# The FFN's last projection: VectorE in written order, free banks first in the third part, GpSimd's share given to VectorE

## The chip, the core and the metric

The kernel runs on one core of a Trainium2 chip. TensorE (PE in the profile) multiplies, VectorE (DVE) and ScalarE (ACT) do elementwise work, GpSimd (POOL) helps them, and the queue of SyncE (SP) issues the loads. Each engine works through its own list of instructions, and semaphores order work between engines. The metric is the device time of one execution in microseconds; the median of three runs of the kernel before is 882.91 us (882.73 to 884.14).

## What is computed

One layer of a streaming encoder on 512 tokens of 1024 features, in float32. Only the last lines are touched by the change: `h` is the residual after attention and recurrence, `w_ffn_out` has 2816 rows.

```python
hn = rmsnorm(h, norm_ffn_g[l])
gu = jnp.einsum('bsd,de->bse', hn, w_ffn_in[l])
g, up = jnp.split(gu, 2, axis=-1)
h = h + (jax.nn.silu(g) * up) @ w_ffn_out[l]
return rmsnorm(h, final_norm_g)
```

## The kernel before

A float32 operand is held as two float32r numbers, a high part (ScalarE's copy, line 82) and the rest (VectorE's subtraction of that copy, line 83). A product of two such operands is three matmuls (`mm3`, lines 76 to 78). So each tile of weights or activations that TensorE reads costs one ScalarE and one VectorE instruction first: `split`. A tile that is first made by a sum (VectorE) and then split goes VectorE, ScalarE, VectorE.

The last projection multiplies activations (512 tokens, four tiles `t` of 128, by 2816 features) with `w_ffn_out`. Its 22 feature tiles are taken in 11 pairs `i`. Pairs 0 to 5, `plain`, are multiplied directly. Pairs 6 to 10, `paired`, go through a seven-product block scheme in place of eight products: the blocks are two halves of the tokens by two feature tiles, and two feature tiles by two halves of the columns. `left` and `right_` are split blocks, or sums of blocks, of the activations; `t12`, `t3b` and `t4` are split sums of blocks of the weights (`out_sums`).

TensorE's order is written out by hand inside `tc.manual_schedule`. It has seven parts: 1. plain pairs, first column half (weights `fo0_0` to `fo0_5`); 2. paired, `fo0_6` to `fo0_10`; 3. plain pairs 0 to 2, second column half (`fo1_0` to `fo1_2`); 4. `t12`; 5. plain pairs 3 to 5 (`fo1_3` to `fo1_5`); 6. `t3b`; 7. `t4`. Sums are kept in PSUM banks: four `po` for the plain pairs, two `pq` and two `qq` for the block products. Each part ends with VectorE's additions of banks to `h` (`h_add`, and `h_out`, which also squares the sum on ScalarE with `accum_out` and multiplies it by the final gain). After part 2 the four `po` banks are used again for the second column half: banks of tokens 2 and 3 are free after part 1, those of tokens 0 and 1 only after part 2.

In the kernel before, the order of the other engines comes from the framework's scheduler, which goes by its own estimate of times; where an instruction stands in an engine's list is then fixed in the program. Tiles come from pools with a few buffers each (weights four and three, raw loads three), and a load waits until the buffer's last reader is done. `weights(name, ahead)` issues loads and splits for `ahead` chunks beyond the one asked for; `spread` hands out listed preparations one or two at a time.

GpSimd's share before: the low parts of the activations of pairs 0, 1, 2 and 4 in `split_act`, and the gain product of tokens 0 and 1 in the first column half (`h_out(..., pool, ...)`).

Of the kernel before, what the change touches and what calls it, by code (L numbers as in the profile page):

```python
# [38 lines left out]
def block_kernel(ctx: ExitStack, tc: tile.TileContext, x, norm_mix_g, w_in, b_merge, rel_table,  # L39
# [28 lines left out]
    def f(ap):  # L68
        return ap.bitcast(F32)
# [999 lines left out]
    def split_act(i):  # L1069
        o = act2[i]  # L1070
        pl, bufs = (acp, 13) if i == 0 else (ohp, OUT_TILES)
        hi = pl.tile([P, 2, S], F32R, tag="act", bufs=bufs, name=f"act_hi{i}")
        lo = acp.tile([P, 2, S], F32R, tag="act", bufs=13, name=f"act_lo{i}")
        act.activation(hi[:], o[:], AF.Copy)  # L1074
        (pool if i in (0, 1, 2, 4) else dve).tensor_sub(lo[:], o[:], f(hi[:]))  # L1075
        for c in range(2):
            actT[2 * i + c] = (hi[:, c], lo[:, c])

# [30 lines left out]
    def a_first(i):  # L1109
        o, left[i] = act2[i], pair_tile(i, "left")  # L1110
        split(left[i][:, :, 0], left[i][:, :, 1], o[:, :, 0:256])

    def a_sums(i):
        o, right_[i] = act2[i], pair_tile(i, "right")
        s = tg_.tile([P, 2, 256], F32, tag="tg", name=f"s_{i}")
        a11, a12, a21, a22 = (o[:, c, t * 256:t * 256 + 256] for t in range(2) for c in range(2))
        dve.tensor_add(s[:, 1], a21, a22)
        dve.tensor_sub(s[:, 0], s[:, 1], a11)
        dve.tensor_sub(a11, a11, a21)
# [15 lines left out]
    def out_block(o, lhs, which, a, w, k, start, at=every):  # L1135
        toks = slice(a * P, (a + 1) * P)
        mm3(o, lhs[:, which, 0, toks], lhs[:, which, 1, toks], w(0, k, at), w(1, k, at), start, False, parts=True)

    def h_add(cc, t, po, at=every):
        hs = ht[t][:, cc * S + at.start:cc * S + at.stop]  # L1140
        dve.tensor_add(hs, po, hs)

    def h_out(cc, t, po, eng, i, at):

        n = slice(cc * S + at.start, cc * S + at.stop)
        hs = ht[t][:, n]
        dve.tensor_add(hs, po[:, 0:at.stop - at.start], hs)  # L1147
        junk = tg_.tile([P, S], F32, tag="tg", name=f"oj{t}_{i}")
        act.activation(junk[:, 0:at.stop - at.start], hs, AF.Square, accum_out=osq[t][:, i:i + 1])
        eng.tensor_mul(hs, hs, g_fin[:, n])  # L1150

    def out_norm(t, parts):

# [18 lines left out]
    def bank(tag, name):  # L1172
        return ps.tile([P, S], F32, tag=tag, bufs=4 if tag == "mm" else 2, name=name)

    def spread(todo, n):

        for _ in range(min(n, len(todo))):
            todo.pop(0)()

    half = N_PLAIN // 2  # L1180
    with tc.manual_schedule(engines={mybir.EngineType.PE}):

        todo = [lambda i=i: a_first(i) for i in paired]
        po = [bank("mm", f"po_out0_{t}") for t in range(NT)]
        for i in plain:
            if i:
                split_act(i)
# [3 lines left out]
            spread(todo, 1)  # L1191
        spread(todo, len(todo))
        for t in (2, 3):
            h_add(0, t, po[t][:])
        pq = [bank("s", f"p_out{a}") for a in range(2)]
        for n, i in enumerate(paired):
            w = weights(f"fo0_{i}", 4)
            for a in range(2):
                out_block(pq[a][:], left[i], 0, a, w, 0, n == 0)
            for a in range(2):  # L1200
                out_block(po[a][:], left[i], 1, a, w, 1, False)
            a_sums(i)
        for a in range(2):
            h_add(0, a, pq[a][:])
            h_out(0, a, po[a], pool, 0, every)
        todo = [lambda i=i: a_second(i) for i in paired]
        po = [bank("mm", f"po_out1_{t}") for t in range(NT)]
        for i in plain[:half]:
            w = weights(f"fo1_{i}", 4)
            for t in range(NT):  # L1210
                out_pair(po[t], t, i, w)
            spread(todo, 2)
        spread(todo, len(todo))

        qq = [bank("t", f"q_out{a}") for a in range(2)]
        for n, i in enumerate(paired):
            w = weights(f"t12_{i}", 4)
            for a in range(2):
                out_block(pq[a][:], right_[i], 0, a, w, 0, False)
            for a in range(2):  # L1220
                out_block(qq[a][:], right_[i], 1, a, w, 1, n == 0)
        for a in range(2):
            h_add(1, a, pq[a][:])
            h_add(1, 2 + a, qq[a][:])
        todo = [lambda i=i: a_last(i) for i in paired]
        for i in plain[half:]:
            w = weights(f"fo1_{i}", 4)
            for t in range(NT):
                out_pair(po[t], t, i, w)
            spread(todo, 2)  # L1230
# [58 lines left out]
```

## Time and profile before

| | us |
|---|---|
| median of three runs | 882.91 |
| the profiled execution | 883.89 |
| its span, first to last instruction | 882.1 |
| TensorE busy in it | 863.6 (98%) |
| VectorE busy | 594.3 (67%) |
| ScalarE busy | 485.9 (55%) |
| GpSimd busy | 112.8 (13%) |

Of the three numbers at the start of a timeline's row the first is the start in us from the span's begin, the second the busy time; a bracket at its end gives the idle time of the engine before it and who ended it. TensorE starts a 128x512 matmul every 0.227 us in the rows although each is shown as 0.39 us long, since matmuls overlap: distances are taken from starts. The table by stretches gives busy time and count per engine and then the granted TensorE clock. The last projection starts at 746.8 us in the span, and its first block of the change at 755.8 us.

### The profile page before, as it was taken

Reading aid. Unit: us, or ns where it says so; the run is one execution under the profiler, and the core shown is the slowest. Engines: PE = TensorE matmul, PEld = TensorE weight load, DVE = VectorE, ACT = ScalarE, POOL = GpSimd, SP = SyncE. Lnnn points to the kernel's source line nnn. Section 1 sums busy time; section 2 is a strip of 40 time slices with the busy share of each in tenths; the row PEclk is TensorE's granted clock in tenths of the full one; section 3 lists DMA queues with packets and bytes.
Section 4 is the critical chain, followed back from the end, with each engine's and each line's share of the span. In section 5 each row is a group of like instructions: output and inputs, shape, how many; then the busy total and the mean of one; then the engine's idle time right before and its main releaser. Section 6 shows DMA issues by size and latency. Waiting matters only on the chain.

```text
span 882.1 us, 13360 instructions
## 1 busy us (share of the span) xinstructions
PE 863.6 (98%) x5139; PEld 768.0 (87%) x5139; DVE 594.3 (67%) x928; ACT 485.9 (55%) x857; POOL 112.8 (13%) x170
## 2 busy tenths in 40 slices
PE   8999999999999999999999999999999999897997
PEld 6988888888889888898888889999999999785886
DVE  5666556663456675766557458888887885888655
ACT  7676556642257675766534367565555655633314
POOL 3612112120112132322000000000000001301000
PEclk9999999999999999999999999999999999998999
DMA  8133232433332332322324532333343332536502
GB/s 288 52 120 99 93 91 79 118 96 96 107 108 72 88 92 74 108 84 61 95 94 155 181 96 72 120 96 97 97 126 113 96 97 95 175 124 199 165 7 95
DMA packets 88303, 95.34 MB, mean 108 GB/s; under 512 B 5696, under 2 KB 74912, under 8 KB 88240
## 3 DMA queue, kind: packets, MB, share of 16 engines
q1 hardware_dynamic: 86640, 90.98, 33.1%
q10 hardware_dynamic: 1376, 3.47, 1.1%
q8 instruction: 40, 0.66, 0.3%
q14 instruction: 23, 0.19, 0.1%
q0 software_dynamic: 224, 0.05, 0.0%
HBM read 92.34 MB, written 2.14 MB: 107 GB/s over the span
## 4 chain that ended last, share of the span: by engine, by line
PE 88%; DVE 6%; ACT 2%; DMA 1%; issue 1%; POOL 1%; DVEq 0%; ACTq 0%; POOLq 0%
PE p_fu L78 2%; PE p_fg L78 2%; PE p_fg L77 2%; PE p_fg L76 2%; PE p_fu L77 2%; PE p_fu L76 2%; PE pT L872 2%; PE o L892 2%; PE po_v L76 2%; PE po_v L78 2%; PE po_v L77 2%; PE po_xr L76 2%; PE po_xr L77 2%; PE po_gr L76 2%; PE po_k L76 2%; PE po_gr L78 2%
## 5 line engine op out<-in xcount | busy, mean ns | idle before, releaser
L861 POOL TENSOR_SCALAR p<-p,rl 128x128 f32<-128x128 f32 (+1 forms) x64 | 36.9, 596 | 134.7 <-DVE rl L859 134.4
L1075 POOL TENSOR_TENSOR act_lo<-act,act_hi 128x1024 fp32r<-128x1024 f32 x4 | 10.5, 2629 | 332.9 <-ACT act_hi L1074 327.0
L76 PE MATMUL po_out<-whl_fo,act_hi 128*128 128x512 f32 x96 | 38.7, 403 | 6.4 <-DVE h L1147 5.9
L858 ACT ACTIVATE p<-p,m 128x128 f32<-128x128 f32 (+1 forms) x64 | 35.7, 560 | 12.1 <-DVE m L857 11.8
L78 PE MATMUL po_out<-whl_fo,act_lo 128*128 128x512 f32 x96 | 38.0, 395 | 1.8 <-POOL act_lo L1075 1.8
L77 PE MATMUL po_out<-whl_fo,act_hi 128*128 128x512 f32 x96 | 37.9, 395 | 0.0
L76 PE MATMUL po_v<-whl_v,xnT 128*128 128x256 f32 x128 | 36.5, 285 | 0.0
L78 PE MATMUL po_v<-whl_v,xnT 128*128 128x256 f32 x128 | 36.2, 283 | 0.0
L77 PE MATMUL po_v<-whl_v,xnT 128*128 128x256 f32 x128 | 36.2, 283 | 0.0
L83 DVE TENSOR_TENSOR whl_qk<-raw_qk,whl_qk 128x1024 fp32r<-128x1024 f32 x16 | 20.9, 1306 | 13.4 <-ACT whl_qk L82 13.4
L857 DVE CUSTOM_DVE_ANT_0 p<-s,bias 128x128 f32<-128x128 f32 (+1 forms) x64 | 29.1, 484 | 1.0 <-PE s L849 1.0
L76 PEld LDWEIGHTS po_out<-whl_fo,act_hi 128*128 128x128 f32 x96 | 18.4, 191 | 11.7 <-DVE h L1147 7.1
L83 DVE TENSOR_TENSOR whl_fu_s<-s_fu,whl_fu_s 128x1024 fp32r<-128x1024 f32 x20 | 24.1, 1222 | 6.2 <-ACT whl_fu_s L82 6.2
L83 DVE TENSOR_TENSOR pp<-pT,pp 128x384 fp32r<-128x384 f32 (+1 forms) x48 | 27.5, 596 | 0.5 <-ACT pp L82 0.4
L77 PE MATMUL po_xr<-xnT,whl_xr 128*128 128x512 f32 (+1 forms) x80 | 27.7, 353 | 0.0
L77 PE MATMUL po_gr<-xnT,whl_gr 128*128 128x512 f32 (+1 forms) x80 | 27.5, 347 | 0.0
L78 PE MATMUL po_gr<-xnT,whl_gr 128*128 128x512 f32 (+1 forms) x80 | 27.3, 347 | 0.0
L78 PE MATMUL po_xr<-xnT,whl_xr 128*128 128x512 f32 (+1 forms) x80 | 27.2, 346 | 0.0
L76 PE MATMUL po_gr<-xnT,whl_gr 128*128 128x512 f32 (+1 forms) x80 | 27.1, 347 | 0.0
L83 DVE TENSOR_TENSOR whl_fg_s<-s_fg,whl_fg_s 128x1024 fp32r<-128x1024 f32 x20 | 24.0, 1222 | 4.2 <-ACT whl_fg_s L82 4.0
L76 PE MATMUL po_xr<-xnT,whl_xr 128*128 128x512 f32 (+1 forms) x80 | 26.3, 351 | 0.4 <-ACT xnT L534 0.4
L83 DVE TENSOR_TENSOR whl_fo<-raw_fo,whl_fo 128x1024 fp32r<-128x1024 f32 x17 | 20.6, 1220 | 9.0 <-ACT whl_fo L82 9.0
(496 smaller groups left out, 3240.9 us busy)
## 6 DMA issues: line engine op xcount, KB each, us to landing
raw_fg<-in_w_ffn_in_dram SPq DMA_DIRECT2D x24, 512.0 KB, 4.0
raw_fu<-in_w_ffn_in_dram SPq DMA_DIRECT2D x22, 512.0 KB, 3.7
raw_fo<-in_w_ffn_out_dram SPq DMA_DIRECT2D x17, 512.0 KB, 3.6
raw_qk<-in_w_in_dram SPq DMA_DIRECT2D x32, 256.0 KB, 3.2
raw_xr<-in_w_in_dram SPq DMA_DIRECT2D x8, 512.0 KB, 3.9
raw_gr<-in_w_in_dram SPq DMA_DIRECT2D x8, 512.0 KB, 3.8
raw_ga<-in_w_in_dram SPq DMA_DIRECT2D x8, 512.0 KB, 3.5
raw_gb<-in_w_in_dram SPq DMA_DIRECT2D x8, 512.0 KB, 3.5
```

The costliest lines, as they stand in the source:

```text
L76: pe.matmul(o, sh, mh, start=start, stop=False, skip_group_check=parts)
L77: pe.matmul(o, sh, ml, start=False, stop=False, skip_group_check=parts)
L78: pe.matmul(o, sl, mh, start=False, stop=stop, skip_group_check=parts)
L83: dve.tensor_sub(lo, src, f(hi))
L857: dve.tensor_tensor_reduce(prob[qb][:], scs[qb][:, 0:w], bias[:, S - w:S], -1.0, 3e38, ALU.add, ALU.min, nmax[:, qb:qb + 1])
L858: act.activation(prob[qb][:], prob[qb][:], AF.Exp, bias=nmax[:, qb:qb + 1], scale=-1.0, accum_out=lsum[:, qb:qb + 1])
L861: pool.tensor_scalar(prob[qb][:], prob[qb][:], rl[:, qb:qb + 1], 1.0, ALU.mult, ALU.mult)
L872: pe.transpose(pt[:, at * P:(at + 1) * P], prob[qb][:, kb * P:(kb + 1) * P], ident[:])
L892: pe.matmul(po[:, S - n:S], st, pp[i][:, part, lo:lo + n], start=kb == 0 and part == 0, stop=kb == NT - 1 and part == 1)
L1075: (pool if i in (0, 1, 2, 4) else dve).tensor_sub(lo[:], o[:], f(hi[:]))
```

## The change

Five things are done to the last projection alone.

1. VectorE's instructions are put under the hand-written order too, so that within this block they stand in the program as the code says. The code is written in another order: `split_act`, `a_first`, `a_sums`, `a_second` and `a_last` stand where VectorE is to do them.
2. GpSimd keeps only `split_act(0)`. The low parts of pairs 1, 2 and 4 and the two gain products (`h_scale`) go to VectorE.
3. In part 3 the first two plain pairs are multiplied for tokens 2 and 3 first, then for tokens 0 and 1.
4. `weights` looks 3 (or 2) chunks ahead where it was 4.
5. The gain products of tokens 0 and 1 move from the end of part 2 into part 5, and the `t4` sums and splits stand ahead of the closing additions.

The diff, cut:

```diff
-        (pool if i in (0, 1, 2, 4) else dve).tensor_sub(lo[:], o[:], f(hi[:]))
+        (dve if i else pool).tensor_sub(lo[:], o[:], f(hi[:]))
...
-    with tc.manual_schedule(engines={mybir.EngineType.PE}):
+    with tc.manual_schedule(engines={mybir.EngineType.PE, mybir.EngineType.DVE}):
...
+            if i + 2 in plain:
+                split_act(i + 2)
+            if n < len(paired):
+                a_first(paired[n])
+            if n:
+                a_sums(paired[n - 1])
...
-            w = weights(f"fo0_{i}", 4)
+            w = weights(f"fo0_{i}", 3)
...
             h_add(0, a, pq[a][:])
-            h_out(0, a, po[a], pool, 0, every)
+            h_sum(0, a, po[a], 0, every)
...
+        first_two = [weights(f"fo1_{i}", 2) for i in plain[:2]]
+
+        for ts in ((2, 3), (0, 1)):
+            for i, w in zip(plain[:2], first_two):
+                for t in ts:
+                    out_pair(po[t], t, i, w)
+        for i in plain[2:half]:
+            w = weights(f"fo1_{i}", 3)
...
-        todo = [lambda i=i: a_last(i) for i in paired]
+        todo = [lambda i=i: a_last(i) for i in paired] + [lambda a=a: h_scale(0, a, dve, every) for a in range(2)]
...
+        ws = [weights(f"t4_{i}", 5) for i in paired]
         for a in range(2):
             h_out(1, 2 + a, pq[a], dve, 0, every)
...
-        ws = [weights(f"t4_{i}", 5) for i in paired]
```

What this does to VectorE's list is shown at three places. The names: `act_lo` is the low part of a plain pair, `whl_...` a split weight tile, `left`/`right` split activations, `s` their sums, `h0` to `h3` the residual of a token tile, `raw_t3b` and `t2` sums of weight blocks.

VectorE at the start of the block, after the last product of the stage ahead (line 1087); before:

```order
L1087 TENSOR_TENSOR act20_7499<-act20_7499,c_u20_7379 128x1024
L83 TENSOR_TENSOR left6_7663<-act12_6523,left6_7663 128x2x256
L1119 TENSOR_TENSOR act12_6523<-act12_6523 128x256
L1120 TENSOR_TENSOR act12_6523<-act12_6523,s_6_7870 128x256
L83 TENSOR_TENSOR whl_fo0_4_7670<-raw_fo0_4_0_7671,whl_fo0_4_7670 128x1024
```

The same place now:

```order
L1087 TENSOR_TENSOR act20_7499<-act20_7499,c_u20_7379 128x1024
L1075 TENSOR_TENSOR act_lo1_7630<-act2_5308,act_hi1_7629 128x1024
L83 TENSOR_TENSOR whl_fo0_2_7633<-raw_fo0_2_0_7634,whl_fo0_2_7633 128x1024
L83 TENSOR_TENSOR whl_fo0_3_7638<-raw_fo0_3_0_7639,whl_fo0_3_7638 128x1024
L1075 TENSOR_TENSOR act_lo2_7668<-act4_5551,act_hi2_7667 128x1024
```

The low part of pair 1 was GpSimd's and now stands right behind that product on VectorE; two weight splits that stood ahead of the product stand behind it.

VectorE at the end of part 2 and the start of part 3, where the additions into `h0` and `h1` free the two banks that TensorE needs; before:

```order
L83 TENSOR_TENSOR left9_7771<-act18_7252,left9_7771 128x2x256
L1141 TENSOR_TENSOR h0_4500<-p_out0_7845,h0_4500 128x512
L83 TENSOR_TENSOR whl_t12_8_8038<-raw_t12_8_8039,whl_t12_8_8038 128x512
L265 TENSOR_TENSOR raw_t12_9_8079<-raw_t12_9_8079 128x512
L1141 TENSOR_TENSOR h1_4501<-p_out1_7846,h1_4501 128x512
L83 TENSOR_TENSOR whl_t12_8_8038<-t2_8_8043,whl_t12_8_8038 128x512
L1147 TENSOR_TENSOR h0_4500<-po_out0_0_7625,h0_4500 128x512
L265 TENSOR_TENSOR raw_t12_10_8119<-raw_t12_10_8119 128x512
```

The same place now:

```order
L83 TENSOR_TENSOR whl_fo1_2_7955<-raw_fo1_2_0_7956,whl_fo1_2_7955 128x1024
L1141 TENSOR_TENSOR h0_4500<-p_out0_7890,h0_4500 128x512
L1146 TENSOR_TENSOR h0_4500<-po_out0_0_7625,h0_4500 128x512
L1141 TENSOR_TENSOR h1_4501<-p_out1_7891,h1_4501 128x512
L1146 TENSOR_TENSOR h1_4501<-po_out0_1_7626,h1_4501 128x512
L265 TENSOR_TENSOR raw_t12_6_7985<-raw_t12_6_7985 128x512
```

The four additions stood among the sums and splits for `t12`; now they stand ahead of all of them.

VectorE at the end, parts 5 to 7; before:

```order
L1141 TENSOR_TENSOR h3_4503<-q_out1_8117,h3_4503 128x512
L83 TENSOR_TENSOR whl_t3b_9_8283<-raw_t3b_9_8284,whl_t3b_9_8283 128x1024
L83 TENSOR_TENSOR whl_t3b_10_8319<-raw_t3b_10_8320,whl_t3b_10_8319 128x1024
L83 TENSOR_TENSOR whl_t4_6_8337<-t2_6_7957,whl_t4_6_8337 128x512
L1141 TENSOR_TENSOR h0_4500<-po_out1_0_7994,h0_4500 128x512
L1141 TENSOR_TENSOR h1_4501<-po_out1_1_7995,h1_4501 128x512
L1141 TENSOR_TENSOR h2_4502<-po_out1_2_7996,h2_4502 128x512
L1141 TENSOR_TENSOR h3_4503<-po_out1_3_7997,h3_4503 128x512
L83 TENSOR_TENSOR whl_t4_7_8355<-t2_7_8003,whl_t4_7_8355 128x512
```

The same stretch now, from the last `t3b`:

```order
L1141 TENSOR_TENSOR h3_4503<-po_out1_3_7983,h3_4503 128x512
L272 TENSOR_TENSOR raw_t3b_10_8320<-raw_t3b_10_8320 128x512
L83 TENSOR_TENSOR whl_t3b_10_8319<-raw_t3b_10_8320,whl_t3b_10_8319 128x1024
L277 TENSOR_TENSOR t2_6_7989<-half_t4_6_8338,t2_6_7989 128x512
L83 TENSOR_TENSOR whl_t4_6_8337<-t2_6_7989,whl_t4_6_8337 128x512
L277 TENSOR_TENSOR t2_7_8049<-half_t4_7_8356,t2_7_8049 128x512
L83 TENSOR_TENSOR whl_t4_7_8355<-t2_7_8049,whl_t4_7_8355 128x512
L277 TENSOR_TENSOR t2_8_8061<-half_t4_8_8374,t2_8_8061 128x512
L83 TENSOR_TENSOR whl_t4_8_8373<-t2_8_8061,whl_t4_8_8373 128x512
```

Each sum (lines 272 and 277) now stands directly ahead of the split that needs ScalarE's copy of that sum; before, the sums for `t4` (line 277) stood in part 3, some 40 us ahead of their splits.

More of the change, by code (lines that the diff above doesn't have):

```diff
@@ L1141, in h_add, with h_sum @@
         dve.tensor_add(hs, po, hs)
-    def h_out(cc, t, po, eng, i, at):
-        n = slice(cc * S + at.start, cc * S + at.stop)
-        hs = ht[t][:, n]
+    def h_sum(cc, t, po, i, at):
+        hs = ht[t][:, cc * S + at.start:cc * S + at.stop]
         dve.tensor_add(hs, po[:, 0:at.stop - at.start], hs)
@@ L1149, in h_out, with h_scale @@
         act.activation(junk[:, 0:at.stop - at.start], hs, AF.Square, accum_out=osq[t][:, i:i + 1])
-        eng.tensor_mul(hs, hs, g_fin[:, n])
+    def h_scale(cc, t, eng, at):
+        n = slice(cc * S + at.start, cc * S + at.stop)
+        eng.tensor_mul(ht[t][:, n], ht[t][:, n], g_fin[:, n])
+    def h_out(cc, t, po, eng, i, at):
+        h_sum(cc, t, po, i, at)
+        h_scale(cc, t, eng, at)
     def out_norm(t, parts):
@@ L1180, in block_kernel @@
     half = N_PLAIN // 2
-    with tc.manual_schedule(engines={mybir.EngineType.PE}):
-        todo = [lambda i=i: a_first(i) for i in paired]
+    with tc.manual_schedule(engines={mybir.EngineType.PE, mybir.EngineType.DVE}):
         po = [bank("mm", f"po_out0_{t}") for t in range(NT)]
-        for i in plain:
-            if i:
-                split_act(i)
+        for n, i in enumerate(plain):
+            if i == 0:
+                split_act(1)
             w = weights(f"fo0_{i}", 3)
@@ L1190, in block_kernel @@
                 out_pair(po[t], t, i, w)
[L1191 to L1195, printed above, removed]
-        for n, i in enumerate(paired):
-            w = weights(f"fo0_{i}", 4)
+            if i + 2 in plain:
[4 more added lines that the diff above has]
+                a_sums(paired[n - 1])
+        for n, i in enumerate(paired):
+            w = weights(f"fo0_{i}", 3)
+            if n == 0:
+                for t in (2, 3):
+                    h_add(0, t, po[t][:])
+                pq = [bank("s", f"p_out{a}") for a in range(2)]
             for a in range(2):
@@ L1201, in block_kernel @@
                 out_block(po[a][:], left[i], 1, a, w, 1, False)
-            a_sums(i)
         for a in range(2):
             h_add(0, a, pq[a][:])
-            h_out(0, a, po[a], pool, 0, every)
-        todo = [lambda i=i: a_second(i) for i in paired]
+            h_sum(0, a, po[a], 0, every)
         po = [bank("mm", f"po_out1_{t}") for t in range(NT)]
-        for i in plain[:half]:
-            w = weights(f"fo1_{i}", 4)
+        first_two = [weights(f"fo1_{i}", 2) for i in plain[:2]]
[5 more added lines that the diff above has]
+            w = weights(f"fo1_{i}", 3)
             for t in range(NT):
                 out_pair(po[t], t, i, w)
-            spread(todo, 2)
-        spread(todo, len(todo))
+        todo = [lambda i=i: a_second(i) for i in paired]
         qq = [bank("t", f"q_out{a}") for a in range(2)]
         for n, i in enumerate(paired):
-            w = weights(f"t12_{i}", 4)
+            w = weights(f"t12_{i}", 3)
             for a in range(2):
@@ L1221, in block_kernel @@
                 out_block(qq[a][:], right_[i], 1, a, w, 1, n == 0)
+            spread(todo, 1)
         for a in range(2):
@@ L1229, in block_kernel @@
                 out_pair(po[t], t, i, w)
-            spread(todo, 2)
+            spread(todo, 3)
         spread(todo, len(todo))
```

## The prediction

> **What bounds the kernel now.** I read the page first, then the table by stretches for the last projection, the list of waits there, and last the order of time of TensorE, VectorE and ScalarE. From the page:
>
> ```profile
> span 882.1 us, 13360 instructions
> PE 863.6 (98%) x5139; PEld 768.0 (87%) x5139; DVE 594.3 (67%) x928; ACT 485.9 (55%) x857; POOL 112.8 (13%) x170
> PE 88%; DVE 6%; ACT 2%; DMA 1%; issue 1%; POOL 1%; DVEq 0%; ACTq 0%; POOLq 0%
> ```
>
> TensorE carries 88% of the chain that ended last. The change adds and takes no matmul, so it can only win time in which TensorE waits, or the tail behind it. The stretches of the last projection (PE, PEld, DVE, ACT, POOL busy, then clock):
>
> ```profile
> 757.80:760.30 2.50, 0.73 (x4) 0.34 (x3) 2.50 (x2) 2.50 (x4) 2.42 (x2) 1.00 0.97 290
> 760.30:802.90 42.60, 42.60 (x190) 35.25 (x188) 35.93 (x48) 20.68 (x29) 5.38 (x2) 1.00 0.46 152
> 802.90:812.80 9.90, 3.96 (x10) 2.37 (x9) 9.90 (x17) 4.15 (x9) 2.71 (x1) 0.66 0.67 223
> 812.80:838.60 25.80, 25.80 (x115) 21.37 (x114) 17.91 (x26) 9.56 (x14) 1.41 (x1) 1.00 0.55 175
> 838.60:868.40 29.80, 29.80 (x134) 24.66 (x133) 13.71 (x21) 6.43 (x10) 0.00 (x0) 1.00 0.00 1
> ```
>
> TensorE is full but for two short stretches. In the second (802.9 to 812.8) VectorE is busy for all 9.90 us: it is late there, while after 838.6 it works less than half the time. The waits:
>
> ```profile
> PE po_out L76 <- DVE h L1147: 5.9, 1, 5.9
> PE po_out L78 <- POOL act_lo L1075: 1.8, 1, 1.8
> ```
>
> TensorE's rows at these places:
>
> ```profile
> 757.75 0.40 PE L77 MATMUL po_out<-whl_fo,act_hi 128*128 128x512 f32 x1
> 759.92 0.50 PE L78 MATMUL po_out<-whl_fo,act_lo 128*128 128x512 f32 x1 [1.77 <-POOL act_lo L1075]
> ...
> 802.90 0.39 PE L78 MATMUL po_out<-whl_fo,act_lo 128*128 128x512 f32 x1
> 809.15 0.79 PE L76 MATMUL po_out<-whl_fo,act_hi 128*128 128x512 f32 x1 [5.86 <-DVE h L1147]
> ...
> 812.16 0.79 PE L76 MATMUL po_out<-whl_fo,act_hi 128*128 128x512 f32 x1
> 838.45 0.39 PE L76 MATMUL po_out<-whl_fo,act_hi 128*128 128x512 f32 x1
> ```
>
> The row at 838.45 is the first matmul of part 5. From 802.90 to it are 121 matmuls (one to end the block, 60 left of part 3's 72 and 60 of part 4); at 0.227 us each they need 27.4 us, and they took 35.55. So the second wait costs 8.1 us in all: 6.0 of waiting, and 2.1 because the six matmuls from 809.15 to 812.16 take 3.0 us where full speed needs 1.4, and a few more are slow.
>
> **The change, step by step.**
>
> *Pair 1's low part (GpSimd to VectorE).* VectorE's rows:
>
> ```profile
> 755.81 1.23 DVE L1087 TENSOR_TENSOR act<-act,c_u 128x1024 f32<-128x1024 f32 x1
> 756.95 0.69 DVE L83 TENSOR_TENSOR left<-act,left 128x512 fp32r<-128x512 f32 x1
> 757.67 2.48 DVE L1119 TENSOR_TENSOR act<-act 128x256 f32<-128x256 f32 x1
> ```
>
> The subtraction takes the place of the row at 756.95, needs 1.22 us as 128x1024 subtractions do, and TensorE goes on at 758.2 in place of 759.92: gain 1.7 us. The two splits now behind it (1.14 us each from start to start) end by 760.5, the low part of pair 2 by 761.7; TensorE wants it at 763.6. The row at 757.67 takes 2.48 us where that form takes 0.42, while GpSimd works: such stretched rows go too, but off TensorE's path.
>
> *The wait in part 3.* VectorE's rows there:
>
> ```profile
> 787.02 0.68 DVE L1141 TENSOR_TENSOR h<-po_out,h 128x512 f32<-128x512 f32 x1
> 791.70 0.69 DVE L265 TENSOR_TENSOR raw_t<-raw_t 128x512 f32<-128x512 f32 x1 [3.99 <-DMA raw_t<-in_w_ffn_out_dram]
> 792.31 0.68 DVE L1141 TENSOR_TENSOR h<-po_out,h 128x512 f32<-128x512 f32 x1
> 798.78 0.69 DVE L265 TENSOR_TENSOR raw_t<-raw_t 128x512 f32<-128x512 f32 x1 [2.32 <-DMA raw_t<-in_w_ffn_out_dram]
> 811.42 0.68 DVE L1147 TENSOR_TENSOR h<-po_out,h 128x512 f32<-128x512 f32 x1
> ```
>
> The additions that free TensorE's banks stand behind sums that wait 3.99 and 2.32 us for loads, and the last ends at 812.1, when TensorE needed it at 804.5. Now the four additions stand ahead of those sums. From the low part at 756.95 to the end of part 2 (796.8 with the first gain) VectorE has 17 instructions of 1.14, 12 of 0.60 and 20 of 0.34 to 0.45: 34.5 us of 39.8, so 5 us are spare. The additions end some 2.5 us behind part 2. Tokens 2 and 3 first gives TensorE 24 matmuls (5.4 us) on free banks where before it had 12 (2.7 us). So I take the whole 8.1 us. Part 4's sums take 3.4 us of VectorE's path per weight block, and TensorE eats one in 2.7, but it starts with a lead of some 11 us, and 7 are left at the fifth. SP's loads for them (issued when their buffers come free, some 790 to 807) land several us ahead of use. Part 5 then starts at 838.45 - 1.7 - 8.1 = 828.65.
>
> *The last parts.* Here VectorE's list is in lockstep with ScalarE: sum, ScalarE's copy, split, next sum. Before, sums stood one or more ahead, so the copies were covered. Rows for a trip, VectorE first, then ScalarE:
>
> ```profile
> 792.91 0.68 DVE L266 TENSOR_TENSOR t<-half_t,raw_t 128x512 f32<-128x512 f32 x1
> 845.23 1.23 DVE L83 TENSOR_TENSOR whl_t3b<-raw_t3b,whl_t3b 128x1024 fp32r<-128x1024 f32 x1 [2.19 <-ACT whl_t3b L82]
> 858.41 0.69 DVE L83 TENSOR_TENSOR whl_t<-t,whl_t 128x512 fp32r<-128x512 f32 x1 [2.03 <-ACT whl_t L82]
> 871.90 0.69 DVE L1150 TENSOR_TENSOR h<-h,g_fin 128x512 f32<-128x512 f32 x1 [0.40 <-ACT oj L1149]
> 876.11 0.41 DVE L1147 TENSOR_TENSOR h<-po_last,h 128x256 f32<-128x256 f32 x1
> 877.63 0.55 DVE L1168 TENSOR_SCALAR h<-h,ors 128x640 f32<-128x640 f32 x1
> ```
>
> ```profile
> 793.70 0.63 ACT L82 ACTIVATE whl_t<-t 128x512 fp32r<-128x512 f32 x1 [0.85 <-DVE t L266]
> 799.65 0.63 ACT L82 ACTIVATE whl_t<-raw_t 128x512 fp32r<-128x512 f32 x1 [4.07 <-DVE raw_t L265]
> 844.14 1.06 ACT L82 ACTIVATE whl_t3b<-raw_t3b 128x1024 fp32r<-128x1024 f32 x1 [4.38 <-PE po_out L78]
> 857.75 0.63 ACT L82 ACTIVATE whl_t<-t 128x512 fp32r<-128x512 f32 x1 [2.09 <-PE q_out L78]
> 869.66 1.28 ACT L1164 ACT_TABLE_LOAD   x1
> 870.96 0.29 ACT L1164 ACTIVATE osd<-osq,part 128x1 f32<-128x1 f32 x1
> 871.16 0.62 ACT L1149 ACTIVATE oj<-h 128x512 f32<-128x512 f32 x1
> 876.56 0.42 ACT L1149 ACTIVATE oj<-h 128x256 f32<-128x256 f32 x1 [0.63 <-DVE h L1147]
> ```
>
> Handing over from VectorE to ScalarE takes 0.04 (876.52 to 876.56), 0.11 (793.59 to 793.70) or 0.18 us (799.47 to 799.65); back it is 0.03 (858.38 to 858.41). A square of 512 releases its product 0.74 after its start (871.16 to 871.90). I take 0.13 for `t3b`, 0.11 for `t4` (nearest form: `whl_t<-t`) and 0.04 for the additions (their own form).
>
> VectorE enters this stretch behind TensorE's last block of part 4: three additions and the hand-over put its first `t3b` sum 1.3 us after part 5 starts, 829.95. Then:
> - five `t3b` trips of 0.69 + 0.13 + 1.06 + 0.03 + 1.15 = 3.06: 15.3
> - five splits of `right` (0.33): 1.7; the two gain products that were GpSimd's (0.60): 1.2; four additions (0.60): 2.4
> - five `t4` trips of 0.68 + 0.11 + 0.63 + 0.03 + 0.63 = 2.08: 10.4. To 860.95.
> - tokens 2 and 3, addition, square, product: 0.68 + 0.04 + 0.74 + 0.62 = 2.08 each: 4.2; two small ones 0.4. To 865.5.
> - token tile 0: addition 0.68, hand-over 0.1, square with its read-out 0.72, table load 1.28, root 0.3, reciprocal 0.2, scaling 0.46, next part 0.07: 3.8
> - tiles 1 and 2: 0.68 + 0.04 + 0.74 + 0.60 + 0.19 + 0.46 + 0.07 = 2.8 and 2.7
> - tile 3: 1.6 for its first 256 columns, 1.5 from the last addition to the last scaling. To 877.95.
>
> The last scaling stands at 877.63 before. From the start of part 5 to it are 39.2 us before, 49.3 now: 10.1 us longer. So 9.8 us won on TensorE are given back, and the end moves by +0.3. TensorE, done with part 6 at 858.65 (132 matmuls, 30.0 us), then waits 3 us for the first closing addition (861.65) to free its bank; its part 7 needs 7 us at full speed. Even if all of it ran as slowly as the six matmuls at 809.15, its last sum would be there at 875, and VectorE wants it at 876.4.
>
> The loads for the fourth and fifth `t4` move on SP from part 3 to behind VectorE's first two `t4` sums, issued near 851.3 and 853.4; such loads land in
>
> ```profile
> half_t<-in_w_ffn_out_dram SPq DMA_DIRECT2D x10, 256.0 KB, 3.9
> ```
>
> 3.9 us, at 855.2 and 857.3, and are used from 856.8 and 858.9: nothing to 1 us. Shallower look-ahead I cost at nothing in parts 1 to 3, covered by VectorE's 5 spare us.
>
> Bounds: all hand-overs at 0.03 take 1.1 us off, all at 0.18 add 1.5; the loads add 0 to 1; the 9.8 is good to 0.3. That is -1.1 to +3.1 around +0.3 at the far ends, about -0.7 to +1.7 for the likely. The profiled execution took 883.89 us (span 882.1), 1.0 above the median, so I set the step on the median: 882.91 + 0.3 = 883.2, its own range 882.2 to 884.6.
>
> The page "TensorE: Matmul & The Clock Gate" of the Trainium skill, section "Architectural detail", speaks against this order: it calls the queues of VectorE and ScalarE strictly first in, first out. By that rule the copies cannot be covered and the sum is mine; without it they could, and the sum would be the second rival's 873.1. The rows agree as far as they go: the addition at 792.31 stayed behind the sum that waited 3.99 us. On the table load page and row differ: "ScalarE: Activation LUTs" of the Trainium skill, section "Step-by-step", gives about 2.7 us including the drain, the row has 1.28; with the page's price for that one step the time would come to 884.6, and I go by the row.
>
> **Rivals.**
> 1. *Slower: each trip costs more.* Sixteen trips now stand on the path. If each hand-over to ScalarE pays the 0.18 seen at 799.65, and each way back the 0.1 that 871.90 shows over the square's end (871.78), that is +1.4 and +0.8: 885.4. For it: rows with several waits pay that. Against: most rows on the way back show 0.03. It decides from 0.1 us per trip.
> 2. *Faster: the copies are covered after all.* Then the last parts keep their 39.2 us and all 9.8 us stay: 873.1. For it: the same instructions took 39.2 before. Against: the list above, in which no sum stands ahead of a waiting split. With half the trips cheaper by 0.4 us it would be 880.
> 3. *The wait in part 3 stays in part.* If VectorE lost more than its 5 us in parts 1 and 2, as it lost 3.99 and 2.32 before, half the wait would stay: +4, 887.2. Against: no load it waits for there is issued late, with 4 us and more from landing to use.
>
> **How the numbers follow.** Forecast 0.60, rival 1 0.19, rival 3 0.07, rival 2 with its halfway cases 0.14. A change of 0.2% (1.8 us) is what a measurement here can tell from none: same 0.60, slower 0.26, faster 0.14. The range leaves out rival 2 whole and rival 3, and takes in rival 1 and the bounds: 881.3 to 885.8.
>
> **What would show it.** Right: TensorE's waits at parts 1 and 3 gone or under 0.6 us; part 5 starting near 828.7; a new wait of some 3 us before `p_out<-whl_t` of part 7, ended by VectorE's `h` at line 1146; VectorE's idle time ended by ScalarE's `whl_t3b` (near 1.2 us each) and `whl_t` (0.8), and the last `h` scaling near 878. Wrong: any of these waits in another place, or the last parts as short as before.

## The result, and the profile after

The changed kernel takes 884.18 us (median of 20 runs, 884.03 to 884.95); the kernel before, run beside it, 883.75 us (882.73 to 884.62). The ratio is 1.0006, 95% interval 0.9999 to 1.0013: plus 0.5 us, between -0.1 and +1.1, and so no change that this measurement can tell from none. The forecast for the change was +0.3. The forecast time, 883.2, lies 1.0 below, most of it from the median that it was set on: 882.91 was a median of three, and twenty runs give 883.75.

The page of the changed kernel, its span, the busy times and the chain that ended last:

```profile
span 882.4 us, 13331 instructions
PE 863.3 (98%) x5139; PEld 768.5 (87%) x5139; DVE 593.6 (67%) x933; ACT 486.7 (55%) x857; POOL 98.6 (11%) x165
PE 93%; DVE 3%; ACT 1%; POOL 1%; issue 1%; DMA 0%; ACTq 0%; DVEq 0%; POOLq 0%
```

Totals and shares hardly differ. The stretches differ much (PE, PEld, DVE, ACT, POOL busy, then clock). The first row is from the second matmul group of part 1 to the end of part 4, the second is parts 5 and 6, the last two are the new wait and what follows it:

```profile
758.20:828.60 70.40, 70.40 (x311) 58.27 (x312) 56.52 (x82) 33.65 (x49) 0.00 (x0) 1.00 0.55 181
828.60:858.30 29.70, 29.70 (x133) 24.55 (x131) 20.51 (x32) 7.84 (x9) 0.00 (x0) 1.00 0.16 54
858.30:861.50 3.20, 0.33 (x2) 0.00 (x0) 2.33 (x4) 0.69 (x2) 0.00 (x0) 0.98 0.00 0
861.50:865.00 3.50, 3.45 (x9) 2.76 (x10) 2.02 (x4) 1.39 (x4) 0.00 (x0) 0.53 0.00 0
```

TensorE has no hole for a hundred us: the wait at 809.15 of before is gone, and the one at 759.92 has shrunk from 1.8 to 0.3 us. Part 5 starts at 828.55 where it started at 838.45. Then TensorE stands still for 3 us at 858.3, and goes on at half clock. Its rows there:

```profile
828.55 0.39 PE L76 MATMUL po_out<-whl_fo,act_hi 128*128 128x512 f32 x1
858.24 0.39 PE L78 MATMUL q_out<-whl_t3b,left 128*128 128x512 f32 x1
861.55 0.77 PE L76 MATMUL p_out<-whl_t,right 128*128 128x512 f32 x1 [2.92 <-DVE h L1146]
```

What it waits for is VectorE's first closing addition, and VectorE's rows say why that comes late (first two trips of `t3b` and `t4`, the first closing addition and its gain product, the last scaling):

```profile
829.87 0.68 DVE L272 TENSOR_TENSOR raw_t3b<-raw_t3b 128x512 f32<-128x512 f32 x1
831.73 1.23 DVE L83 TENSOR_TENSOR whl_t3b<-raw_t3b,whl_t3b 128x1024 fp32r<-128x1024 f32 x1 [1.18 <-ACT whl_t3b L82]
832.88 0.69 DVE L272 TENSOR_TENSOR raw_t3b<-raw_t3b 128x512 f32<-128x512 f32 x1
...
850.35 0.69 DVE L277 TENSOR_TENSOR t<-half_t,t 128x512 f32<-128x512 f32 x1
851.82 0.69 DVE L83 TENSOR_TENSOR whl_t<-t,whl_t 128x512 fp32r<-128x512 f32 x1 [0.78 <-ACT whl_t L82]
852.43 0.68 DVE L277 TENSOR_TENSOR t<-half_t,t 128x512 f32<-128x512 f32 x1
...
860.72 0.68 DVE L1146 TENSOR_TENSOR h<-p_out,h 128x512 f32<-128x512 f32 x1
862.20 0.69 DVE L1153 TENSOR_TENSOR h<-h,g_fin 128x512 f32<-128x512 f32 x1 [0.79 <-ACT oj L1148]
...
877.93 0.55 DVE L1175 TENSOR_SCALAR h<-h,ors 128x640 f32<-128x640 f32 x1
```

Each bracket is VectorE standing between a sum and the piece that needs ScalarE's answer to it. From its list of waits:

```profile
DVE whl_t3b L83 <- ACT whl_t3b L82: 6.1, 5, 1.3
DVE whl_t L83 <- ACT whl_t L82: 3.9, 5, 0.8
DVE h L1153 <- ACT oj L1148: 5.3, 7, 0.8
```

So 15.3 us of VectorE's time from part 5 on are waits of this one kind, and its last scaling stands at 877.93 where before it stood at 877.63.

### The profile page after: what moved, and what is told of

Its sections match the earlier page's. It is cut to its first block, busy times and chain, and to the rows that moved or that the text cites. A ratio compares the mean times of both kernels' runs of the same rounds, so it can differ in the third digit from the quotient of the medians.

```text
span 882.4 us, 13331 instructions
## 1 busy us (share of the span) xinstructions
PE 863.3 (98%) x5139; PEld 768.5 (87%) x5139; DVE 593.6 (67%) x933; ACT 486.7 (55%) x857; POOL 98.6 (11%) x165
## 4 chain that ended last, share of the span: by engine, by line
PE 93%; DVE 3%; ACT 1%; POOL 1%; issue 1%; DMA 0%; ACTq 0%; DVEq 0%; POOLq 0%
PE po_out L78 3%; PE po_out L76 3%; PE po_out L77 3%; PE p_fu L78 2%; PE p_fg L77 2%; PE p_fg L76 2%; PE p_fu L77 2%; PE p_fg L78 2%; PE p_fu L76 2%; PE pT L872 2%; PE o L892 2%; PE po_v L76 2%; PE po_v L78 2%; PE po_v L77 2%; PE po_xr L76 2%; PE po_xr L77 2%
## 5 line engine op out<-in xcount | busy, mean ns | idle before, releaser
L1075 POOL TENSOR_TENSOR act_lo<-act,act_hi 128x1024 fp32r<-128x1024 f32 x1 | 2.4, 2410 | 300.7 <-ACT act_hi L1074 300.7
L82 ACT ACTIVATE whl_qk<-raw_qk 128x1024 fp32r<-128x1024 f32 x16 | 16.8, 1052 | 17.5 <-PE po_yb L78 10.4
```

Of the source, the lines that this page charges most:

```text
L82: act.activation(hi, src, AF.Copy)
L1075: (dve if i else pool).tensor_sub(lo[:], o[:], f(hi[:]))
```

## The experiments

The theory: the 9.8 us that TensorE wins in parts 1 and 3 are real, and VectorE's written order takes them back in parts 5 to 7, since each sum stands directly ahead of the piece that waits for ScalarE's copy or square of it. The rivals: the last parts need their 49 us in any order; the gain was lost for another reason (GpSimd's share moved, late loads); a fixed order costs by itself. Each kernel was measured beside the kernel before on the same chip; there that took 883.8 to 884.1 us.

| run | us | ratio to before (95%) |
|---|---|---|
| sums one ahead | 880.15 | 0.9960 (0.9948 to 0.9973) |
| closing part interleaved | 880.03 | 0.9953 (0.9940 to 0.9965) |
| both | 876.00 | 0.9915 (0.9901 to 0.9928) |
| both, last tiles too | 874.52 | 0.9890 (0.9875 to 0.9905) |
| written order only to part 4 | 874.13 | 0.9892 (0.9877 to 0.9907) |
| before, with the last parts of the change | 892.52 | 1.0095 (1.0081 to 1.0108) |
| plain token order in part 3 | 884.19 | 1.0004 (0.9995 to 1.0013) |
| GpSimd's share given back | 884.40 | 1.0002 (0.9993 to 1.0011) |
| `t4` behind the closing additions | 886.07 | 1.0022 (1.0013 to 1.0031) |
| before, low parts on VectorE | 879.00 | 0.9950 (0.9936 to 0.9963) |
| the same, GpSimd busy beside it | 885.83 | 1.0026 (1.0015 to 1.0037) |

**The sums one ahead.** In `out_sums`, for `t3b` and `t4`, ScalarE's copy follows its sum at once, and VectorE's subtraction is kept back until the next sum has been issued:

```diff
+    def split_later(hi, lo, src):
+        act.activation(hi, src, AF.Copy)
+        pay()
+        owed.append((lo, src, f(hi)))
...
-            split(hl[:, 0], hl[:, 1], raw[:])
+            split_later(hl[:, 0], hl[:, 1], raw[:])
...
-            split(hl[:, 0, 0], hl[:, 1, 0], t2[:])
+            split_later(hl[:, 0, 0], hl[:, 1, 0], t2[:])
...
         ws = [weights(f"t4_{i}", 5) for i in paired]
+        pay()
```

> The changed kernel with one edit: each sum for `t3b` and `t4` stands one ahead of the split before it, so that ScalarE copies sum i+1 while VectorE splits i; the closing additions keep their order. My theory (the lockstep of sum, copy and split gives the won 9.8 us back) expects: VectorE's idle time ended by ScalarE's `whl_t3b` and `whl_t` in the last parts, 6.1 and 3.9 us in the changed kernel, goes down to under 2 us together; TensorE's wait of 2.92 us before part 7 is gone; the closing chain, still in lockstep, starts with the first closing sum near 856.5 in place of 860.7, since the banks are full only then; the last scaling comes 4.1 us earlier, near 873.8, and the time is 880.1 (879.3 to 881). The rival that the copies were not what took the time, and that the closing parts need their length from the start of part 5 in any order, expects no change: 884.2, and the last scaling near 878.

880.15. The waits for the two copies, 10.0 us in the changed kernel, are nearly gone, and VectorE now stands idle for the first closing addition until the bank is full (its waits):

```profile
DVE whl_t3b L247 <- ACT whl_t3b L250: 0.6, 1, 0.6
DVE whl_t L247 <- ACT whl_t L250: 0.2, 1, 0.2
DVE h L1156 <- PE p_out L78: 1.7, 1, 1.7
DVE h L1163 <- ACT oj L1158: 5.3, 7, 0.8
```

The closing chain's waits, 5.3 us, are what they were, and it starts at 856.61 in place of 860.72; the last scaling moves by the same 4.1 us, to 873.82. The order of the sums is thus a cause, and one of two.

**The closing part alone.** Both sums of tokens 2 and 3 first, then those of tokens 0 and 1, each gain product behind the next sum; the trips stay:

```diff
         for a in range(2):
-            h_out(1, 2 + a, pq[a], dve, 0, every)
+            h_sum(1, 2 + a, pq[a], 0, every)
         h_add(0, 3, pq[1][:, CW:S], slice(CW, S))
+        part2 = [out_norm(a, 1) for a in range(2)]
         for a in range(2):
-            part = out_norm(a, 1)
-            h_out(1, a, qq[a], dve, 1, every)
-            h_norm(a, part, 1)
+            h_sum(1, a, qq[a], 1, every)
+            h_scale(1, 2 + a, dve, every)
+        for a in range(2):
+            h_scale(1, a, dve, every)
+            h_norm(a, part2[a], 1)
```

> The changed kernel with the closing additions alone taken out of lockstep (both sums of tokens 2 and 3, then both of tokens 0 and 1, each gain product behind the next sum); the `t3b` and `t4` trips stay as the change has them. My theory expects the trips to cost what they cost in the changed kernel (TensorE waits 2.9 us before part 7, first closing sum near 860.7) and the closing chain to be about 4 us shorter: last scaling near 873.8, time 880.0 (879.3 to 880.7). With the sums ahead alone 4.0 us came back and with both 8.2: if the two parts add, this one alone gives 4.1. The rival that the closing edit only works where VectorE enters it early expects under 2 us: 882.2 or more.

880.03: 4.1 us less than the changed kernel, with the trips and TensorE's wait as they were.

**Both.**

> The run with the `t3b` and `t4` sums one ahead, and the closing additions of the column half taken out of lockstep as well: both sums of tokens 2 and 3, then both of tokens 0 and 1, each gain product behind the next sum. My theory expects that the rest of the 9.8 us comes back: TensorE is full from part 5 to its last matmul, VectorE's last scaling near 868.5 to 869.3, time 874.5 to 875.5. The rival that the closing chain is bound by ScalarE's squares and not by VectorE's order expects the 880.1 of the run with the sums alone.

876.00: 8.2 us less, the sum of the two edits (4.0 and 4.1), but 0.5 above the range given. What is left stands at the end: the last two token tiles still go sum, square, product, scaling one after the other (its rows for tile 2):

```profile
864.41 0.68 DVE L1156 TENSOR_TENSOR h<-p_out,h 128x512 f32<-128x512 f32 x1
866.06 0.69 DVE L1163 TENSOR_TENSOR h<-h,g_fin 128x512 f32<-128x512 f32 x1 [0.97 <-ACT oj L1158]
```

**All of it written by hand.** `h_norm` is cut in two, the root with its reciprocal and the scalings, and a tile's scaling stands behind the next tile's sum:

```diff
-        h_out(0, 2, pq[0], dve, 1, every)
-        h_norm(2, part, 1)
+        h_sum(0, 2, pq[0], 1, every)
+        h_last(1, r1)
...
-        h_out(0, 3, pq[1], dve, 1, slice(0, CW))
+        h_sum(0, 3, pq[1], 1, slice(0, CW))
+        h_scale(0, 2, dve, every)
+        r2 = h_root(2, part, 1)
+        h_scale(0, 3, dve, slice(0, CW))
...
+        h_last(2, r2)
```

> The run with both edits (sums one ahead, closing additions out of lockstep), with the last two token tiles taken out of lockstep too: the scaling of a tile stands behind the next tile's sum, as the scheduler has it in the run whose written order ends before part 5. All of VectorE's order is written by hand. My theory (it is which instruction stands next, not that the order is fixed) expects the rest of the gain: last scaling near 868, time 874.1 (873.5 to 874.7). The rival that a written order of VectorE itself costs something in these parts expects to stay at 875 to 876.

874.52, last scaling at 868.35: 9.7 us under the changed kernel, all with VectorE's order fixed. VectorE's order is as fixed here as in the changed kernel, so a fixed order does not cost the 9.7 us; at most the 0.4 us between this and the next run are left for it.

**The written order only up to part 4.** A second block, with TensorE's order alone, begins ahead of part 5:

```diff
+    with tc.manual_schedule(engines={mybir.EngineType.PE}):
+
         todo = [lambda i=i: a_last(i) for i in paired] + [lambda a=a: h_scale(0, a, dve, every) for a in range(2)]
```

> The changed kernel with VectorE's written order ended before part 5: parts 1 to 4 are as in the changed kernel, and from part 5 on VectorE's order is the framework scheduler's again (it puts the `t4` sums far ahead and the closing sums ahead of the gain products). My theory expects that all of the 9.8 us won in parts 1 and 3 stay: part 5 starts near 828.6 as in the changed kernel, no wait of TensorE before part 7, last scaling near 868, time 874.4 (873.4 to 875.4). The rival that something else behind part 5 was lost (the two gain products of 1.2 us now on VectorE, or `t4` loads that land late) expects 875.5 to 884; that the tail needs its 49 us however VectorE is ordered, 884.2.

874.13, the fastest of all. TensorE is full from 828.7 to 863.7, and the last scaling stands at 867.85:

```profile
828.70:863.70 35.00, 35.00 (x163) 29.28 (x162) 24.93 (x40) 13.84 (x23) 0.00 (x0) 1.00 0.17 57
```

The last parts are 39.2 us from the start of part 5 (828.66) again, as before the change, and the whole gain stays: 10.0 us against the changed kernel, where the prediction's working gave 9.8 won and 10.1 lost. In the same parts VectorE waits for ScalarE's `whl_t` for 5.0 us and TensorE does not wait at all: there the scheduler does the `t4` sums early, and VectorE has time.

**The other half.** The kernel before up to part 4, the changed kernel's code and written order from part 5 on:

> The other half: parts 1 to 4 as in the kernel before (GpSimd's share, the scheduler's order, the wait in part 3), and parts 5 to 7 in the changed kernel's written order. My theory expects the loss without the gain: TensorE waits 1.8 and 5.9 us in parts 1 and 3 as before, part 5 starts near 838.4, VectorE takes up part 5's last addition near 855.2 and needs from there 0.6 + 3.1 (the fifth `t3b`) + 10.4 (five `t4` trips) + 17.2 (the closing chain as it took in the changed kernel, 860.72 to 877.93): last scaling near 886.5, time 892.6 (891.5 to 893.5). The rival that the order of the last parts costs nothing by itself, and that what was won in parts 1 to 3 went for another reason, expects 883.8.

892.52, and 892.6 was expected. Nothing was won ahead, and the loss stands alone. In part 1 TensorE waits 1.8 us for GpSimd's low part, as before; its waits at part 3 and ahead of part 7 are:

```profile
PE po_out L76 <- DVE h L1147: 4.3, 1, 4.3
PE p_out L76 <- DVE h L1147: 1.3, 1, 1.3
```

The wait at part 3 is 4.3 us and not the 5.9 expected, since TensorE comes to it 1.6 us later (804.51 against 802.90): in the profiled execution eight matmuls in part 1 came at half speed. It ends where it ended before, at 809.2.

This and the run ahead of it take the change apart: against the kernel before, the front alone is worth -9.7 us (874.13 beside 883.83) and the back alone +8.4 (892.52 beside 884.08); with the 1.2 us of gain products, which GpSimd still does in the second of them, the sum is -0.1, within half a microsecond of the +0.4 that the whole change measures.

**Token order in part 3.**

```diff
-        for ts in ((2, 3), (0, 1)):
-            for i, w in zip(plain[:2], first_two):
-                for t in ts:
-                    out_pair(po[t], t, i, w)
+        for i, w in zip(plain[:2], first_two):
+            for t in range(NT):
+                out_pair(po[t], t, i, w)
```

> The changed kernel with part 3 multiplied for all four token tiles of a pair in turn, as before the change. The additions that free the two banks end near 798.84 and 800.23 in the changed kernel, and TensorE starts part 3 at 798.63; with 12 matmuls on the first free banks it needs the third bank 2.7 us later, near 801.35. The theory that the additions' place ahead of the `t12` sums alone took the 8.1 us away, and the order of tokens nothing, expects no wait of TensorE over 0.3 us in part 3, part 5 from 828.6, and 884.2 (883.9 to 884.5). The rival that the free banks first do a part of it expects a wait of 0.5 to 2.7 us at part 3 and an end as much later, 884.7 to 886.9.

884.19, and no wait in part 3. In the changed kernel the two additions stand here, and part 3 starts at 798.63:

```profile
798.15 0.69 DVE L1146 TENSOR_TENSOR h<-po_out,h 128x512 f32<-128x512 f32 x1 [0.67 <-PE po_out L78]
798.76 0.68 DVE L1141 TENSOR_TENSOR h<-p_out,h 128x512 f32<-128x512 f32 x1
799.54 0.69 DVE L1146 TENSOR_TENSOR h<-po_out,h 128x512 f32<-128x512 f32 x1
```

They end at 798.84 and 800.23; the 12 matmuls that are free in any case last until 801.35. The lead that the new token order gives is never used: "free banks first", one of the parts that the title names, does nothing here.

**GpSimd's share given back**, in `split_act` and for the two gain products:

> The changed kernel with GpSimd's share given back: the low parts of pairs 1, 2 and 4 and the two gain products of the first column half. My theory expects TensorE's wait in part 1 to be back (1.3 to 1.8 us in place of 0.3 and 0.7), part 5 to start 1.5 us later, near 830.1, and VectorE's last parts to be 1.2 us shorter without the two products: 0.3 to 0.5 later in all, 884.5 to 884.7. The rival that GpSimd beside VectorE stretches VectorE's rows (2.48 for 0.42 us at one place before the change) enough to hold up the last parts expects 886 or more.

884.40. TensorE waits 1.5 us for GpSimd's low part again and part 5 starts 1.3 us later, at 829.86; VectorE's last parts are 1.2 us shorter, and the end is 0.2 later, 0.1 less than the least expected. The wait in part 3 does not come back, although GpSimd stretches VectorE's rows again (one of 1.22 us takes 3.43 at 759.85).

**The `t4` weights behind the closing additions.**

```diff
-        ws = [weights(f"t4_{i}", 5) for i in paired]
         for a in range(2):
             h_out(1, 2 + a, pq[a], dve, 0, every)
...
+        ws = [weights(f"t4_{i}", 5) for i in paired]
         for w, i in zip(ws, paired):
```

> The changed kernel with the line that asks for the `t4` weights put back behind the closing additions of the second column half. By the look-ahead of four blocks four of the five `t4` sums and splits still stand ahead of them; the fifth stands behind. My theory (VectorE's list is one chain in these parts, so that a shift within it only matters where TensorE waits for the shifted piece) expects TensorE's first wait before part 7 to shrink from 2.9 to about 1 us, a second wait of some 9 us for the fifth `whl_t`, and an end 1 to 2 us later: 885.7 (885.0 to 886.5). The rival that TensorE's wait before part 7 is what sets the end expects 1 to 2 us less: 882 to 883.

886.07. TensorE stands still for 8.8 us, by its list of waits, and the end moves by 1.9:

```profile
PE p_out L76 <- ACT whl_t L82: 8.8, 1, 8.8
PE p_out L76 <- DVE h L1146: 0.8, 1, 0.8
```

TensorE, busy for 98% of the span, stands still for 6.7 us more than in the changed kernel (9.6 against 2.9), and the end moves by less than a third of that: VectorE goes on with its own chain meanwhile, and loses only the 1.25 us that its sum at 873.29 then waits for TensorE's late matmuls. In this written order, having the fifth `t4` ahead of the closing additions is worth the 1.9 us.

**The low parts on VectorE, nothing else**, in the kernel before:

```diff
-        (pool if i in (0, 1, 2, 4) else dve).tensor_sub(lo[:], o[:], f(hi[:]))
+        (dve if i else pool).tensor_sub(lo[:], o[:], f(hi[:]))
```

> The kernel before with one edit: the low parts of pairs 1, 2 and 4 on VectorE in place of GpSimd, everything else as before. The prediction counted 1.7 us for this in part 1. My theory expects TensorE's wait in part 1 to shrink by 0.5 to 1.7 us, but VectorE, late in part 3 before (5.9 us) and 3.6 us fuller now, to hand it back there: a wait of 6 to 9 us in part 3 and 883.3 to 885. The rival that the 1.7 us are won whatever follows expects 882.0.

879.00: 5.1 us under the kernel before, which neither side expected. TensorE's wait in part 1 shrank by only 0.3 us (1.77 to 1.47), since the scheduler puts the low part of pair 1 behind three other rows; the gain is in part 3. The rows here are from an execution of 881.82, in which eleven matmuls of part 3 came at half speed; three of the five executions lie within 0.1 of 879. VectorE did more, and was done earlier. Its rows at the place where the prediction had seen 2.48 us for 0.42, and the two additions in part 3:

```profile
757.62 0.42 DVE L1119 TENSOR_TENSOR act<-act 128x256 f32<-128x256 f32 x1
757.96 0.42 DVE L1120 TENSOR_TENSOR act<-act,s 128x256 f32<-128x256 f32 x1
...
804.36 0.69 DVE L1147 TENSOR_TENSOR h<-po_out,h 128x512 f32<-128x512 f32 x1
...
807.37 0.69 DVE L1147 TENSOR_TENSOR h<-po_out,h 128x512 f32<-128x512 f32 x1
```

The second addition stood at 811.42 before: it is 4.05 us earlier. In the kernel before, GpSimd's first row ran from 757.50 to 759.87, and three of VectorE's rows had been stretched, the one at 757.67 and these two:

```profile
760.07 2.63 DVE L1120 TENSOR_TENSOR act<-act,s 128x256 f32<-128x256 f32 x1
...
769.16 2.90 DVE L83 TENSOR_TENSOR left<-act,left 128x512 fp32r<-128x512 f32 x1
```

Against 0.42, 0.42 and 0.69 that is 6.5 us too long in all; three subtractions of 1.14 cost 3.4, so VectorE should be 3.1 us earlier. The scheduler also chose another order for VectorE, which is a rival, but the rows leave it little room. From the product at 755.8 to the end of its last weight split ahead of the additions VectorE does the same instructions in both runs, but for the three low parts, and stands idle for under 0.3 us in each; another order of the same work cannot save time there. That split ends at 787.10 before and at 783.73 here, 3.4 us earlier. The load for the first `t12` sum waits for it and is issued right behind it (787.13 and 783.75). From the first addition on VectorE's list is the same in both runs, and the additions come 4.05 us earlier; the 0.7 beyond 3.4 lies in how long the loads for those sums took to land.

**GpSimd busy beside it.** The run ahead, with GpSimd doing the same three subtractions once more into the room of the final gain, which is loaded after them:

```diff
+        if i in (1, 2, 4):
+            pool.tensor_sub(g_room[0][:], o[:].rearrange("p a b -> p (a b)"), f(hi[:]).rearrange("p a b -> p (a b)"))
```

> The run with the low parts of pairs 1, 2 and 4 on VectorE, with GpSimd made to do the same three subtractions beside it into a place that nobody reads (the room of the final gain, which is loaded after them). VectorE's work is the same as without them. The theory formed on that run, which came out 4.9 us under the kernel before: GpSimd stretches the VectorE rows that fall beside it (2.06, 2.21 and 2.21 us too long at three places before the change) by more than the three subtractions cost on VectorE (3.4 us), and that made VectorE late in part 3. It expects rows of 2 us and more beside GpSimd again, the additions that free the banks about 6 us later, and 884 to 887. The rival that the gain came from the scheduler's other order and not from GpSimd's silence expects 879.0.

885.83, inside the range. GpSimd's first row, VectorE's beside it, and TensorE's wait for the low part of pair 1:

```profile
757.39 2.54 POOL L1078 TENSOR_TENSOR g_fin<-act,act_hi 128x1024 f32<-128x1024 f32 x1 [26.14 <-ACT act_hi L1075]
```

```profile
757.74 2.47 DVE L1122 TENSOR_TENSOR act<-act 128x256 f32<-128x256 f32 x1
760.14 2.58 DVE L1123 TENSOR_TENSOR act<-act,s 128x256 f32<-128x256 f32 x1
762.64 1.21 DVE L1076 TENSOR_TENSOR act_lo<-act,act_hi 128x1024 fp32r<-128x1024 f32 x1
763.78 3.42 DVE L83 TENSOR_TENSOR whl_fo<-raw_fo,whl_fo 128x1024 fp32r<-128x1024 f32 x1
...
813.51 0.68 DVE L1150 TENSOR_TENSOR h<-po_out,h 128x512 f32<-128x512 f32 x1
```

```profile
763.91 0.80 PE L78 MATMUL po_out<-whl_fo,act_lo 128*128 128x512 f32 x1 [5.82 <-DVE act_lo L1076]
```

Work that nobody reads moves VectorE's addition from 807.37 to 813.51 and the time by 6.8 us. Three VectorE rows (2.47, 2.58 and 3.42 for 0.42, 0.42 and 1.22) are stretched by 6.4 us together; the first ends only behind GpSimd's own row, which ends at 759.93. The page "SBUF — State Buffer" of the Trainium skill, section "Who interferes with whom", has this rule: a VectorE instruction with two inputs in SBUF contends with a GpSimd instruction that reads SBUF, and the later one is blocked for the whole of the other. These rows agree with it.

The stretching is thus seen again, but the way from it to the time is not the one that the theory had, and that the 6 us at the additions came out is luck. Here the low part of pair 1 stands on VectorE behind two of the stretched rows (762.64), and TensorE waits 5.8 us for it in part 1, where it waited 1.5 without GpSimd; up to that row VectorE's order is the same in the two runs. TensorE is 5.7 us late from there on (808.29 against 802.55 at its last matmul ahead of the wait in part 3), VectorE waits for it at the end of part 1, and the wait in part 3 is no longer than in the run ahead (2.6 against 2.2 and 1.0). So this run shows that work on GpSimd can cost VectorE and the kernel several microseconds. That the stretched rows made VectorE late in part 3 before the change rests on the count of rows in the run ahead.

## Why the prediction was right, and where it was not

*Part 1, 1.7 us won.* TensorE was to go on at 758.2; it did at 758.11.

*Part 3, 8.1 us won.* Part 5 was to start at 828.65; it started at 828.55. The sum held, one half of its reason did not. The lead by the token order was counted as part of it and is worth nothing (884.19 without it); VectorE's additions came sooner than thought, 1.6 us behind part 2 and not 2.5. And the prediction set the stretched rows aside as "off TensorE's path". They were on it: before the change they held VectorE up by 6.5 us, and with it the loads that its sums in part 3 wait for. The run with the low parts alone is free of them, does 3.4 us more on VectorE, and has the additions 4.05 us earlier, half of the 8.1. In this change that made no difference to the time, since the written order, which puts the additions ahead of the sums, removes the wait with GpSimd's share in place as well (884.40). One more reading was off: of the 2.1 us put down to slow matmuls, 0.3 is a second wait, for the addition that starts at 811.42 and ends at 812.10.

*The five spare us of VectorE in parts 1 and 2.* It stood idle for 5.0 us in the last stretch ahead of part 3 (1.30, 1.35 and 2.31), so the spare was there.

*The last parts, 10.1 us longer.* The first `t3b` sum was forecast for 829.95 and stood at 829.87; a `t3b` trip at 3.06 and took 3.01; a `t4` trip at 2.08 and took 2.08; the first closing sum at 860.95 and stood at 860.72; the last scaling at 877.95 and stood at 877.93. The hand-overs were thus sized rightly, and the first rival, 0.1 us more per trip, had no ground. The loads for `t4` cost nothing, the low end of what was allowed: no sum of `t4` waits for one.

*TensorE's new wait.* Forecast 3 us, over at 861.65; it was 2.92, over at 861.55. Part 7 ran slow for eight matmuls only, and its last sum was there by 870.3, 6 us ahead of use.

*The rivals.* Nothing speaks for the second any more: with VectorE's order as written the copies cannot be covered, and where the order lets them be covered the time comes to 874.1 to 874.5, as that rival priced it within 1.5 us of its 873.1 (0.8 of that is the median it was set on). The third would have shown as a wait in part 3, and there is none.

Whether the change as a whole costs the 0.5 us of the medians stays open: its interval reaches to -0.1. The shallower look-ahead, priced at nothing, was not taken out by itself in any run.

## What to carry to other kernels

Where a list is fixed, look in each loop for a piece that waits for another engine's answer to the piece directly ahead of it, and put the next round's first piece between them; here that was worth 9.7 us of 884, and the same engine's busy share (67%) showed none of it. A gain on the busiest engine counts only up to the next chain that ends at the same time, so add up that chain before and after as well. And before work is given to GpSimd beside VectorE, compare VectorE's own rows with and without it: three helpers that took 3.4 us off VectorE cost it 6.5.

## What the runs showed of the hardware that was not expected

GpSimd's stretching of VectorE rows was seen ahead of the change, but not its size against the help: see the last two runs. It can also hit GpSimd: in the run with the last parts of the change GpSimd's third row, at 768.21, took 5.05 us where the others took 2.4 to 2.5, and VectorE's rows beside it kept their length.

After idle times of the same length TensorE does not always fall to half clock. From start to start the hole ahead of part 7 is 3.31 us in the changed kernel, and eight matmuls behind it are slow, most of them 0.43 us apart; it is 3.29 us in the run with the closing part alone, and there only the first step, 0.31 us, is longer than the 0.23 of full speed:

```profile
861.71 0.47 PE L76 MATMUL p_out<-whl_t,right 128*128 128x512 f32 x1 [2.91 <-DVE h L1146]
862.02 0.39 PE L77 MATMUL p_out<-whl_t,right 128*128 128x512 f32 x1
862.25 0.40 PE L78 MATMUL p_out<-whl_t,right 128*128 128x512 f32 x1
```

The page "TensorE: Matmul & The Clock Gate" of the Trainium skill, section "HAM oscillation — how this bites in real kernels", warns of idle gaps of more than some 3.4 us. The two holes lie just under that figure and came out differently, and shorter ones did too: the 2.17 us at 759.92 in the kernel before slowed one matmul, but a hole of 2.16 us at the same place, in the run with the last parts of the change, was followed by eight slow ones. The 6.25 us at 809.15 slowed seven. So these runs bear out no sharp limit; what decides below it stays open.
